# One traced order for every engine queue, with five to eight raw weight buffers and LayerNorm in place, in a two-layer encoder

## The chip, the core and the metric

The kernel runs on one core of a Trainium2 chip. The metric is the device time of one execution, in microseconds. Before the change the median of three runs is 1156.98 us (1156.47 to 1160.61). The execution that the profiler recorded took 1159.23 us, 2.25 us more than that median; all rows below come from it.

## What is computed

Two layers on x (256 tokens, 1024 channels). Each layer is a half-step SwiGLU FFN (inner width 2816), a token mixer, and a second half-step FFN, each followed by a LayerNorm of the scaled residual. The mixer of layer 0 is multi-scale pooling, that of layer 1 a dilated attention with 16 heads of 64 in three dilation groups.

```python
def reference(x, ...):
    for i in range(DEPTH):
        h = _swiglu(x, ffn1_w_gate[i], ffn1_w_up[i], ffn1_w_down[i])
        x = _layer_norm(ALPHA * x + MACARON_WEIGHT * h, ln_gain[i, 0], ln_bias[i, 0])
        if i % N_MIXERS == 0:
            m = _pool_mixer(x, pool_w_in[p], pool_w_group[p], pool_scale[p], pool_w_out[p])
        else:
            m = _dilated_attention_mixer(x, attn_w_qkv[a], attn_w_out[a])
        x = _layer_norm(ALPHA * x + m, ln_gain[i, 1], ln_bias[i, 1])
        h = _swiglu(x, ffn2_w_gate[i], ffn2_w_up[i], ffn2_w_down[i])
        x = _layer_norm(ALPHA * x + MACARON_WEIGHT * h, ln_gain[i, 2], ln_bias[i, 2])
    return x
```

## The kernel before

Every product is taken in three parts: each float32 operand is split into a rounded high half and the remainder, and high times high, high times low and low times high are added in PSUM. For the weights this happens on the chip. A **unit** of weights is 128 x 2048 numbers and arrives in two **half blocks** of 128 x 1024 (512 KB): SyncE (SP) issues the load into a buffer `raw` (L109), ScalarE (ACT) casts it to the high half (L84), VectorE (DVE) subtracts that from `raw` to get the low half (L85), and only then may `raw` take the next load. There are three `raw` buffers (`N_RAW = 3`), four places `w` for split units, three `d` and one `dlast` for the down weights of an FFN.

An FFN loops over 22 blocks f of 128 inner channels. A block takes one `gate/up` unit: 16 wide products (`mm_wide`, L124 with 512 columns and L125 with 256), eight into one PSUM bank for the gate and eight into another for the up part. `join` copies half of a bank to SBUF on ACT (L129) and adds the other half on DVE (L130); then come the SiLU on ACT, the multiplication on DVE and the split into `hTh` and `hTl`. The banks called `mm` are two, so the products of the next block wait until the `join` of the block before has read its bank. The down products (`down`, three instructions each, L116 to L118, made by `mm3`) of an earlier block stand between the wide ones. The first block of the first FFN takes a transposed copy of x, which `load_first` brings in five pieces (one, one, two, two and two eighths), each with the same eighths of the first unit.

In the attention, each pair of heads has its wide products for q and k, and the values of pairs 2 to 7 are products of three instructions. `scores`, `transposed` and `weighted` of a pair are put off and run a given number of products later (`AT_LEFT`, `stepped`), that is, among the values of the next pair. The cleared halves of `kbh` and `kbl` hold the keys of groups 1 and 2. The last pair has no next one: its score products, transposes and weighted sums come when the loop has ended, ahead of `project_out`.

The order of the instructions is the tile scheduler's: it takes the program text as priorities and moves an instruction past others that are not ready in its own simulation, on each engine by itself.

Of the kernel before, what the change touches and what calls it, by code (L numbers as in the profile page):

```python
# [40 lines left out]
N_RAW = 3  # L41


AT_PROJ = (KT, KT + 1)
N_EARLY = 0
# [5 lines left out]


def _alibi(h):
    return 2.0 ** (-8.0 * (h + 1) / (N_GROUPS * N_HEADS))


@with_exitstack
def tile_trunk(ctx: ExitStack, tc: tile.TileContext, x, x_t, ffn_gu, ffn_d, ln_p, pool_in, pool_group,
               pool_scale, pool_out, attn_qk, attn_v, attn_out, ident_c, dist_c, qscale_c,
               window_c, out):  # L60
    nc = tc.nc

    const = ctx.enter_context(tc.tile_pool(name="const", bufs=1))
    wpool = ctx.enter_context(tc.tile_pool(name="wpool", bufs=4))
    xpool = ctx.enter_context(tc.tile_pool(name="xpool", bufs=1))
    lnpool = ctx.enter_context(tc.tile_pool(name="lnpool", bufs=2))
    small = ctx.enter_context(tc.tile_pool(name="small", bufs=4))
    psum = ctx.enter_context(tc.tile_pool(name="psum", bufs=2, space=PSUM))

    def bank(tag):  # L70
        return psum.tile([P, 512], F32, tag=tag, name=tag, bufs=4 if tag == "acc" else 2)

    def banks():
        return [bank("acc") for _ in range(2)]

    ident = const.tile([P, P], F32, name="ident")
    neg_half = const.tile([P, 1], F32, name="neg_half")
    nc.vector.memset(neg_half, -0.5)


    def split(hi, lo, src, scale=None):

        if scale is None:
            return (nc.scalar.copy(out=hi, in_=src),  # L84
                    nc.vector.tensor_tensor(out=lo, in0=src, in1=hi.bitcast(F32), op=ALU.subtract))  # L85
        return (nc.scalar.activation(out=hi, in_=src, func=AF.Copy, scale=scale),
                nc.vector.scalar_tensor_tensor(out=lo, in0=src, scalar=scale, in1=hi.bitcast(F32),
                                               op0=ALU.mult, op1=ALU.subtract))

    @contextmanager  # L90
    def behind(instructions):

        with ExitStack() as bctx:
            for ins in instructions or ():
                bctx.enter_context(tc.issue_after(ins.ins))
            yield

    def load_unit(src, pool=None, tag="w", n=2048, cuts=1):

        pool = pool or wpool  # L100
        both = pool.tile([P, 2, 2048], F32R, tag=tag, name=tag)
        hi, lo = both[:, 0], both[:, 1]
        half = n // 2
        for i in range(2):
            raw = wpool.tile([P, 1024], F32, tag="raw", name="raw", bufs=N_RAW)
            for j in range(cuts):
                r = slice(j * half // cuts, (j + 1) * half // cuts)
                s = slice(i * half + r.start, i * half + r.stop)
                nc.sync.dma_start(out=raw[:, r], in_=src[:, s])  # L109
                split(hi[:, s], lo[:, s], raw[:, r])  # L110
        return hi, lo

    def mm3(o, lhs, rhs, first, last):

        (lh, ll), (rh, rl) = lhs, rhs
        nc.tensor.matmul(o, lhsT=lh, rhs=rh, start=first, stop=False)  # L116
        nc.tensor.matmul(o, lhsT=lh, rhs=rl, start=False, stop=False)  # L117
        nc.tensor.matmul(o, lhsT=ll, rhs=rh, start=False, stop=last)  # L118

    def mm_wide(o, w, xs, first, last):  # L120


        wh, wl = w
        nc.tensor.matmul(o, lhsT=wh, rhs=xs, start=first, stop=False)  # L124
        nc.tensor.matmul(o[:, S:], lhsT=wl, rhs=xs[:, :S], start=False, stop=last)  # L125

    def join(out, o):

        nc.scalar.copy(out=out, in_=o[:, S:])  # L129
        nc.vector.tensor_tensor(out=out, in0=o[:, :S], in1=out, op=ALU.add)  # L130

    def ln_params(i):
        gb = lnpool.tile([P, 2, D], F32, tag="gb", name="gb", bufs=1)
        nc.sync.dma_start(out=gb, in_=ln_p[i:i + 1].broadcast_to([P, 2, D]))
        return gb

    def new_xT():

        xT = xpool.tile([P, KT, 2 * S], F32R, tag="xT", name="xT")
        return xT[:, :, :S], xT[:, :, S:], xT  # L140

    def transpose_x(y, xT, tt, b):

        ts = slice(tt * P, (tt + 1) * P)
        bs = slice(b * 4, (b + 1) * 4)
        tr = bank("tr").rearrange("p (k t) -> p k t", k=4)
        for k in range(4):
            c = b * 4 + k
            nc.tensor.transpose(tr[:, k, :], y[:, c * P:(c + 1) * P], ident)
        return split(xT[0][:, bs, ts], xT[1][:, bs, ts], tr)  # L150

    def layer_norm(acc, weight, before, gb):
# [4 lines left out]
        y = lnpool.tile([P, D], F32, tag="y", name="y", bufs=4)  # L157
        least = min(a.shape[1] for a in acc)
        stats = small.tile([P, 4, 6], F32, tag="stats", name="stats", bufs=2)
        pieces = []  # L160
        at = 0
        for a in acc:
            s = slice(at, at + a.shape[1])
            pieces.append(s)
            nc.vector.scalar_tensor_tensor(out=y[:, s], in0=before[:, s], scalar=ALPHA / weight, in1=a,
                                           op0=ALU.mult, op1=ALU.add)
            for c in range(s.start, s.stop, least):
                nc.vector.bn_stats(out=stats[:, c // least, :], in_=y[:, c:c + least])
            at = s.stop
        mv = small.tile([P, 2], F32, tag="mv", name="mv")  # L170
# [615 lines left out]
```

## Time and profile before

| | us |
|---|---|
| median of three runs | 1156.98 |
| the profiled execution | 1159.23 |
| its span | 1157.5 |
| TensorE busy (PE) | 1108.6 |
| VectorE busy (DVE) | 777.0 |
| ScalarE busy (ACT) | 623.2 |
| mean granted clock of TensorE, share of full speed | 0.992 |

By the timeline, the stages stand at about: FFN of layer 0 4 to 203 us, pooling to 250 and its output projection to 275, second FFN to 465, first FFN of layer 1 to 661, attention to 937, its output projection to 960, last FFN to 1150. Busy shares are averages over these stages. A row of the timeline ends with the idle time of the engine just before the instruction and what ended it. Products overlap by their fill time, so a stretch in which TensorE is shown fully busy can still hold short waits.

### The profile page before, as it was taken

To read this page: it belongs to the slowest core of one execution; us is meant where nothing else is said; L and a number is where in the kernel's file an instruction comes from. 1 tells how busy PE (TensorE), PEld (TensorE's weight loads), DVE (VectorE), ACT (ScalarE), POOL (GpSimd) and SP (SyncE) were. 2 spreads that over 40 slices of the span, in tenths; PEclk is the share of its full clock that TensorE was granted. 3 is DMA by queue.
4 is the path that set the end of the run, shared out by engine and by line. 5 is a ranking of instruction groups with operands and counts; after the bars stand their busy time and mean duration, and the time that the engine had idled before them with its cause. 6 is when DMAs were issued, how large, how long until landed. Compare 5 with 4: busy or idle time off the path is not lost.

```text
span 1157.5 us, 16223 instructions
## 1 busy us (share of the span) xinstructions
PE 1108.6 (96%) x6164; PEld 950.3 (82%) x6164; DVE 777.0 (67%) x1341; ACT 623.2 (54%) x1130; POOL 16.5 (1%) x32
## 2 busy tenths in 40 slices
PE   7989989999999999999998999999999999999997
PEld 6878878878778877988887897988988878888876
DVE  6676657578665656666556659888888877656555
ACT  5665454254554553455445358777777745545440
POOL 0000000000000000000000110000000000000000
PEclk9999989999999999999999999999999999999999
DMA  8765554165655554465555344444445436655421
GB/s 274 255 237 200 200 180 166 57 216 205 223 202 190 181 179 150 145 236 201 176 188 183 123 143 167 141 147 140 142 155 167 151 117 218 227 200 181 171 104 37
DMA packets 57534, 201.80 MB, mean 174 GB/s; under 512 B 6640, under 2 KB 7536, under 8 KB 56688
## 3 DMA queue, kind: packets, MB, share of 16 engines
q1 hardware_dynamic: 57456, 200.77, 50.8%
q8 instruction: 48, 0.79, 0.3%
q14 instruction: 30, 0.25, 0.1%
HBM read 199.70 MB, written 1.05 MB: 173 GB/s over the span
## 4 chain that ended last, share of the span: by engine, by line
DMA 31%; PE 27%; ACT 18%; DVE 18%; issue 6%; SPq 0%; DVEq 0%; ACTq 0%
DMA raw<-in_ffn_d_dram 15%; DMA raw<-in_ffn_gu_dram 14%; DVE w L85 8%; PE mm L124 7%; ACT w L84 7%; ACT d L84 4%; PE mm L125 4%; DVE d L85 3%; PE acc L116 3%; PE acc L118 3%; PE acc L117 3%; PE mm L118 1%; PE mm L117 1%; PE mm L116 1%; DMA raw<-in_pool_out_dram 1%
## 5 line engine op out<-in xcount | busy, mean ns | idle before, releaser
L124 PE MATMUL mm<-xT,w 128*128 128x512 f32 x1456 | 529.9, 405 | 30.8 <-DVE up L130 18.8
L125 PE MATMUL mm<-xT,w 128*128 128x256 f32 x1456 | 410.5, 283 | 0.3 <-DVE w L85 0.3
L85 DVE TENSOR_TENSOR w<-raw,w 128x1024 fp32r<-128x1024 f32 (+3 forms) x277 | 322.7, 1173 | 86.2 <-ACT w L84 81.5
L124 PEld LDWEIGHTS mm<-xT,w 128*128 128x128 f32 x1456 | 276.7, 190 | 107.7 <-DVE up L130 24.8
L84 ACT CAST w<-raw 128x1024 fp32r<-128x1024 f32 (+3 forms) x277 | 275.6, 1010 | 81.8 <-DMA raw<-in_ffn_gu_dram 63.8
L125 PEld LDWEIGHTS mm<-xT,w 128*128 128x128 f32 x1456 | 279.0, 192 | 2.5 <-DVE w L85 0.6
L85 DVE TENSOR_TENSOR d<-raw,d 128x1024 fp32r<-128x1024 f32 x100 | 122.0, 1225 | 163.7 <-ACT d L84 163.0
L84 ACT CAST d<-raw 128x1024 fp32r<-128x1024 f32 x100 | 104.4, 1049 | 146.8 <-DMA raw<-in_ffn_d_dram 132.7
L118 PE MATMUL acc<-d,hTl 128*128 128x512 f32 (+1 forms) x316 | 121.7, 385 | 1.0 <-DVE hTl L85 1.0
L116 PE MATMUL acc<-d,hTh 128*128 128x512 f32 (+1 forms) x316 | 122.1, 386 | 0.0
L117 PE MATMUL acc<-d,hTh 128*128 128x512 f32 (+1 forms) x316 | 121.6, 385 | 0.0
L118 PEld LDWEIGHTS acc<-d,hTl 128*128 128x128 f32 x316 | 59.3, 188 | 14.6 <-DVE hTl L85 2.5
L124 PE MATMUL acc<-xT,w 128*128 128x512 f32 x192 | 70.4, 402 | 0.0
L116 PEld LDWEIGHTS acc<-d,hTh 128*128 128x128 f32 x316 | 59.4, 188 | 13.1 <-ACT hTh L84 0.3
L246 ACT ACTIVATE h<-h 128x256 f32<-128x256 f32 x79 | 32.9, 417 | 68.9 <-DVE h L130 68.9
L117 PEld LDWEIGHTS acc<-d,hTh 128*128 128x128 f32 x316 | 59.4, 188 | 10.0
L130 DVE TENSOR_TENSOR up<-mm,up 128x256 f32<-128x256 f32 x79 | 33.3, 421 | 38.7 <-ACT up L129 38.7
L116 PE MATMUL mm<-w,xT 128*128 128x384 f32 (+1 forms) x176 | 56.9, 323 | 0.6 <-ACT v L508 0.3
L117 PE MATMUL mm<-w,xT 128*128 128x384 f32 (+1 forms) x176 | 56.5, 321 | 0.0
L118 PE MATMUL mm<-w,xT 128*128 128x384 f32 (+1 forms) x176 | 56.5, 321 | 0.0
L125 PE MATMUL acc<-xT,w 128*128 128x256 f32 x192 | 54.2, 282 | 0.0
L84 ACT CAST hTh<-h 128x256 fp32r<-128x256 f32 x79 | 31.9, 404 | 29.5 <-DVE h L247 29.5
(168 smaller groups left out, 1385.0 us busy)
## 6 DMA issues: line engine op xcount, KB each, us to landing
raw<-in_ffn_gu_dram SPq DMA_DIRECT2D x172, 512.0 KB, 4.5
raw<-in_ffn_d_dram SPq DMA_DIRECT2D x88, 512.0 KB, 4.2
raw<-in_attn_qk_dram SPq DMA_DIRECT2D x48, 512.0 KB, 3.8
raw<-in_attn_v_dram SPq DMA_DIRECT2D x32, 384.0 KB, 3.2
gb<-in_ln_p_dram SPq DMA_DIRECT2D x6, 1024.0 KB, 4.8
raw<-in_pool_in_dram SPq DMA_DIRECT2D x8, 512.0 KB, 3.6
raw<-in_pool_out_dram SPq DMA_DIRECT2D x8, 512.0 KB, 4.7
raw<-in_attn_out_dram SPq DMA_DIRECT2D x8, 512.0 KB, 3.7
```

What stands on the lines that cost most here:

```text
L84: return (nc.scalar.copy(out=hi, in_=src), nc.vector.tensor_tensor(out=lo, in0=src, in1=hi.bitcast(F32), op=ALU.subtract))
L85: nc.vector.tensor_tensor(out=lo, in0=src, in1=hi.bitcast(F32), op=ALU.subtract))
L116: nc.tensor.matmul(o, lhsT=lh, rhs=rh, start=first, stop=False)
L117: nc.tensor.matmul(o, lhsT=lh, rhs=rl, start=False, stop=False)
L118: nc.tensor.matmul(o, lhsT=ll, rhs=rh, start=False, stop=last)
L124: nc.tensor.matmul(o, lhsT=wh, rhs=xs, start=first, stop=False)
L125: nc.tensor.matmul(o[:, S:], lhsT=wl, rhs=xs[:, :S], start=False, stop=last)
L130: nc.vector.tensor_tensor(out=out, in0=o[:, :S], in1=out, op=ALU.add)
L246: nc.scalar.activation(out=out, in_=ps_g, func=AF.Silu)
```

## The change

The tile scheduler is switched off (`manual_schedule`): each engine issues in the order in which the program traces its instructions. A class `Order` decides that order with a timeline of its own. The products are traced in program order. Before each of them, everything that starts earlier by that timeline is traced: **jobs** (the copies, joins, activations and splits that follow a product) and weight operations. A cast or subtract of weights is passed over while a job of the same engine is due before 0.4 of its duration has gone. Weights are one list for the whole program; loads, casts and subtracts follow the list, each as far ahead as buffers allow.

The `raw` buffers become five, with three more (`rawx`) in the FFN and projection stages. The place `dlast` is gone, and units of gate/up weights may lie in `w` or `d`. LayerNorm writes over the residual in two tiles `y` instead of four. Products and their arithmetic are the same. The diff touches the whole file; this is its core:

```diff
-N_RAW = 3
+N_RAW = 5
+N_RAW_MORE = 3
...
+class Order:
...
+    def _next(self):
+        best = None
+        soon = {}
+        for j in self.jobs:
+            engine, us, fn = j.ops[j.at]
+            if any(not a.done for a in j.after):
+                continue
+            start = max([self.free[engine], j.ready] + [a.ready for a in j.after])
+            soon[engine] = min(soon.get(engine, 1e9), start)
+            if best is None or start < best[0]:
+                best = (start, 0, lambda j=j, start=start: self._job(j, start))
+        for start, engine, us, fn in self._weights():
+            if engine in soon and soon[engine] < start + 0.4 * us:
+                continue
+            if best is None or start < best[0]:
+                best = (start, 1, fn)
+        return best
...
+    def need(self, *jobs):
+        for j in jobs:
+            if j is not None:
+                self.until(lambda: j.done)
+                self.pe = max(self.pe, j.ready)
...
+    def product(self, us, fn):
+        self.advance(self.pe)
+        fn()
+        self.pe += us
...
+    ctx.enter_context(tc.manual_schedule())
...
-            raw = wpool.tile([P, 1024], F32, tag="raw", name="raw", bufs=N_RAW)
...
-        y = lnpool.tile([P, D], F32, tag="y", name="y", bufs=4)
...
-            last_place = fctx.enter_context(tc.tile_pool(name="dlast", bufs=1, side="right", reuse_waits="tile"))
...
+        raw_x, raw_w = q.raws[0:2], q.raws[2:4]
+        for ks in (1, 1, 2, 2, 2):
...
+            nc.sync.dma_start(out=rx, in_=x_t[:, s])
+            nc.sync.dma_start(out=rw, in_=ffn_gu[0, 0][:, s])
...
+            j = job(ops[0], ops[2], ops[1], ops[3])
...
+            if at == 1024 or at == 2048:
+                need(j)
+                raw_x[at // 1024 - 1].free = raw_w[at // 1024 - 1].free = j.ready
```

What this moves, at three places.

**The start, SP's queue.** `x_t` is the transposed input, `ffn_gu` the gate/up weights and `ffn_d` the down weights of the first FFN. Before:

```order
L670 DMA y<-in_x_t_dram 128x256
L671 DMA raw<-in_ffn_gu_dram 128x256
L670 DMA y<-in_x_t_dram 128x256
L671 DMA raw<-in_ffn_gu_dram 128x256
L670 DMA y<-in_x_t_dram 128x512
L671 DMA raw<-in_ffn_gu_dram 128x512
L670 DMA y<-in_x_t_dram 128x512
L671 DMA raw<-in_ffn_gu_dram 128x512
L670 DMA y<-in_x_t_dram 128x512
L671 DMA raw<-in_ffn_gu_dram 128x512
L109 DMA raw<-in_ffn_gu_dram 128x512 x4
L109 DMA raw<-in_ffn_d_dram 128x1024 x2
```

After:

```order
L952 DMA raw_87<-in_x_t_dram 128x256
L953 DMA raw_89<-in_ffn_gu_dram 128x256
L952 DMA raw_87<-in_x_t_dram 128x512
L953 DMA raw_89<-in_ffn_gu_dram 128x512
L161 DMA raw_91<-in_ffn_gu_dram 128x1024
L161 DMA rawx_110<-in_ffn_gu_dram 128x1024
L161 DMA rawx_111<-in_ffn_d_dram 128x1024
L161 DMA rawx_112<-in_ffn_d_dram 128x1024
L952 DMA raw_88<-in_x_t_dram 128x512
L953 DMA raw_90<-in_ffn_gu_dram 128x512
L952 DMA raw_88<-in_x_t_dram 128x512
L953 DMA raw_90<-in_ffn_gu_dram 128x512
```

Four half blocks of the second gate/up unit and the first down unit now stand ahead of the last two pieces of the input and of the first unit (x_t 128x512 twice, ffn_gu 128x512 twice). ACT and DVE have their four casts and subtracts at the same place of their queues.

**The attention, TensorE, the scores of one token half of a pair among the values of the next pair** (`kbh`, `kbl` are the split keys of groups 1 and 2, `mm<-w,xT` a values product). Before:

```order
L117 MATMUL acc<-kbl_5732,qh 128x2x128
L118 MATMUL acc<-kbh_5731,ql 128x2x128
L116 MATMUL mm<-w,xT 128x384
L116 MATMUL acc<-kbh_5737,qh 128x2x128
L117 MATMUL mm<-w,xT 128x384
L118 MATMUL mm<-w,xT 128x384
L116 MATMUL mm<-w,xT 128x384
L117 MATMUL mm<-w,xT 128x384
L118 MATMUL mm<-w,xT 128x384
L116 MATMUL mm<-w,xT 128x384
L117 MATMUL mm<-w,xT 128x384
L117 MATMUL acc<-kbl_5738,qh 128x2x128
```

After:

```order
L775 MATMUL acc_78<-k_5830,qh_5792 128x256
L777 MATMUL acc_78<-k_5830,q0l_5022 128x256
L775 MATMUL acc_78<-k_5830,qh_5792 128x256
L777 MATMUL acc_78<-k_5830,q0l_5022 128x256
L318 MATMUL acc_75<-kbh_5010,qh 128x2x128
L319 MATMUL acc_75<-kbl_5011,qh 128x2x128
L320 MATMUL acc_75<-kbh_5010,ql 128x2x128
L318 MATMUL acc_75<-kbh_5016,qh 128x2x128
L319 MATMUL acc_75<-kbl_5017,qh 128x2x128
L320 MATMUL acc_75<-kbh_5016,ql 128x2x128
L318 MATMUL mm_80<-w_85,xT 128x384
L319 MATMUL mm_80<-w_85,xT 128x384
```

Before, eight instructions of values products stand between the score products of group 1 (`kbl_5732` is its low part) and the `kbl` product of group 2, one of them ahead of that group's first product. Now the six score products of groups 1 and 2 are next to each other, and the values products come after them. This is pair 2; pairs 3 to 6 read alike, and in pairs 0 and 1 the six stand next to each other in both kernels.

**The end of the attention, TensorE, the last pair** (`mm<-w,oTh` is a product of `project_out`, `tr<-ident,s` a transpose, `tr<-ph,v` a weighted sum). Before:

```order
L116 MATMUL mm<-w,oTh_5702 128x512
L117 MATMUL mm<-w,oTh_5702 128x512
L116 MATMUL acc<-kbh_5725,qh 128x2x128 x2
L118 MATMUL mm<-w,oTl_5703 128x512
L116 MATMUL mm<-w,oTh_5704 128x512
L117 MATMUL mm<-w,oTh_5704 128x512
L118 MATMUL mm<-w,oTl_5705 128x512
L116 MATMUL mm<-w,oTh_5706 128x512
L117 MATMUL acc<-kbl_5726,qh 128x2x128
L118 MATMUL acc<-kbh_5725,ql 128x2x128
L117 MATMUL acc<-kbl_5726,qh 128x2x128
L118 MATMUL acc<-kbh_5725,ql 128x2x128
```

After:

```order
L820 MATMUL tr_81<-ident,s 128x128 x3
L835 MATMUL tr_82<-ph,v_7444 128x256
L835 MATMUL tr_82<-pl,v_7444 128x256
L835 MATMUL tr_82<-ph,v_7509 128x256
L844 MATMUL tr_82<-p_7723,v_1_5029 64x64 x4
L835 MATMUL tr_82<-pl,v_7509 128x256
L835 MATMUL tr_82<-ph,v_7444 128x256
L835 MATMUL tr_82<-pl,v_7444 128x256
L835 MATMUL tr_82<-ph,v_7509 128x256
L844 MATMUL tr_82<-p_7726,v_1_5029 64x64 x4
L835 MATMUL tr_82<-pl,v_7509 128x256
L318 MATMUL mm_79<-w_86,oTh_4984 128x512
```

Before, twelve products of `project_out` stand between the last pair's scores, transposes and weighted sums, and three of their instructions already between its scores. Now the first one comes when the last weighted sum has been issued.

## Rows read from the trace of the kernel before

**Rows 1.** Page, part 1: busy time, share of the span, instructions of each engine.

```profile
PE 1108.6 (96%) x6164; PEld 950.3 (82%) x6164; DVE 777.0 (67%) x1341; ACT 623.2 (54%) x1130; POOL 16.5 (1%) x32
```

**Rows 2.** Waits of TensorE: instruction waiting <- releaser: us in total, times, longest us.

```profile
PE mm L124 <- DVE up L130: 18.8, 15, 3.2
...
PE mm L124 <- DVE h L130: 4.6, 8, 1.5
...
PE acc L116 <- ACT kbh L643: 1.6, 4, 0.7
...
PE acc L117 <- DVE kbl L646: 1.2, 1, 1.2
```

**Rows 3.** Timeline, two wide products one after the other (line, form).

```profile
156.29 0.40 PE L124 MATMUL mm<-xT,w 128*128 128x512 f32 x1
...
156.64 0.39 PE L124 MATMUL mm<-xT,w 128*128 128x512 f32 x1
```

**Rows 4.** Timeline, 160 to 168 us: start us, us, engine, line, [idle before <-releaser].

```profile
160.07 7.49 SPq L109 DMA_DIRECT2D raw<-in_ffn_d_dram  x2
...
164.90 1.04 ACT L84 CAST d<-raw 128x1024 fp32r<-128x1024 f32 x1 [3.73 <-DMA raw<-in_ffn_d_dram]
...
167.59 0.80 PE L124 MATMUL mm<-xT,w 128*128 128x512 f32 x1 [3.16 <-DVE up L130]
```

**Rows 5.** Timeline, after another wait of the same kind, in the last FFN.

```profile
1113.63 0.50 PE L124 MATMUL mm<-xT,w 128*128 128x512 f32 x1 [2.44 <-DVE up L130]
```

**Rows 6.** Windows: us, busy of PE, PEld, DVE, ACT, POOL; PEclk, DMA share, GB/s.

```profile
8.00:10.00 2.00, 1.70 (x5) 1.53 (x6) 2.00 (x4) 1.89 (x4) 0.00 (x0) 1.00 1.01 370
166.40:173.20 6.80, 5.61 (x17) 4.84 (x18) 5.63 (x8) 3.86 (x7) 0.00 (x0) 0.50 0.63 212
627.20:630.60 3.40, 3.40 (x12) 2.84 (x11) 2.56 (x5) 1.78 (x4) 0.00 (x0) 0.50 0.76 259
709.10:712.50 3.40, 3.40 (x13) 2.92 (x12) 3.05 (x14) 3.23 (x7) 0.00 (x0) 0.50 0.51 204
1113.60:1120.40 6.80, 6.77 (x38) 5.89 (x39) 5.56 (x9) 3.58 (x8) 0.00 (x0) 1.00 0.22 77
920.00:940.00 20.00, 19.84 (x113) 15.04 (x111) 14.13 (x47) 10.08 (x25) 0.00 (x0) 1.00 0.32 103
```

**Rows 7.** Timeline of the start, around the fifth eighth of the first product.

```profile
8.14 0.62 ACT L84 CAST xT<-y 128x512 fp32r<-128x512 f32 x1
...
9.72 0.63 PE L124 MATMUL mm<-xT,w 128*128 128x512 f32 x1
```

**Rows 8.** Timeline, second-group scores next to the first's: pairs 0 (707) and 1 (731).

```profile
707.08 0.39 PE L116 MATMUL acc<-kbh,qh 128*128 128x256 f32 x1 [0.67 <-ACT kbh L643]
...
708.72 0.39 PE L117 MATMUL acc<-kbl,qh 128*128 128x256 f32 x1 [1.25 <-DVE kbl L646]
...
731.23 0.29 PE L117 MATMUL acc<-kbl,qh 128*128 128x256 f32 x1
```

**Rows 9.** Timeline, pair 2: the same key product with a values product before it.

```profile
762.28 0.39 PE L116 MATMUL acc<-kbh,qh 128*128 128x256 f32 x1 [0.46 <-ACT kbh L643]
```

**Rows 10.** Timeline, TensorE through the last pair of the attention.

```profile
921.34 0.28 PE L125 MATMUL acc<-xT,w 128*128 128x256 f32 x1
...
933.54 0.52 PE L549 MATMUL tr<-ident,s 128*128 128x128 f32 x3
...
936.53 0.68 PE L569 MATMUL tr<-p,v 128*64 128x64 f32 x8
```

**Rows 11.** Timeline, one project_out product of three and the next one's start.

```profile
943.17 0.39 PE L116 MATMUL acc<-w,oTh 128*128 128x512 f32 x1
...
943.87 0.39 PE L116 MATMUL acc<-w,oTh 128*128 128x512 f32 x1
```

**Rows 12.** Page, part 5: group xcount | busy us, mean ns | idle before, releaser.

```profile
L85 DVE TENSOR_TENSOR d<-raw,d 128x1024 fp32r<-128x1024 f32 x100 | 122.0, 1225 | 163.7 <-ACT d L84 163.0
...
L130 DVE TENSOR_TENSOR up<-mm,up 128x256 f32<-128x256 f32 x79 | 33.3, 421 | 38.7 <-ACT up L129 38.7
```

More of the change, by code (lines that the diff above doesn't have):

```diff
@@ L90, in behind @@
[L90 to L104, printed above, removed]
-            raw = wpool.tile([P, 1024], F32, tag="raw", name="raw", bufs=N_RAW)
[L106 to L111, printed above, removed]
+    gb = lnpool.tile([P, 2, D], F32, name="gb")
@@ new lines, in finish_last, with gu_unit, d_unit @@
+    def finish_last(steps, weight):
+        for tt in range(2):
+            ln = LayerNorm(ys[tt], weight, 512 if tt == 0 else 256)
+            for b in steps(tt):
+                if b is not None:
+                    ln.piece(*b)
+            for s, done in zip(ln.pieces, ln.end()):
+                need(done)
+                nc.sync.dma_start(out=out[tt * P:(tt + 1) * P, s], in_=ys[tt][:, s])
+    def gu_unit(i, f):
+        return Unit(ffn_gu[i, f], 2048, ("w", "d"))
+    def d_unit(i, f):
+        return Unit(ffn_d[i, f], 2048, ("d",) if f > (NFF - N_HELD) // 2 - 1 else ("d", "w"))
@@ L328, in ffn @@
-                    join(up, parts[1])
-                    gate(h, up, h)
-                    split(hT[f][0], hT[f][1], h)
-                down_unit(f)
-                if f == 6:
-                    gb = ln_params(n_ln)
-                    if first:
-                        load_x(ys)
-                while n_major <= f and done < min(f, NFF - N_HELD):
-                    for tt in range(2):
-                        for j in range(len(acc[tt])):
-                            down(done, tt, j)
-                    done += 1
@@ new lines, in ffn @@
+            hT[f] = places[f % n_places]
+            ready[f] = job(dve(S, lambda h=h: nc.vector.tensor_tensor(out=h, in0=h, in1=up, op=ALU.mult)),
+                           *split(*hT[f], h, S), after=jobs)
+            if f == 6:
+                ln_params(n_ln)
+                if first:
+                    load_x()
+            while n_major <= f and done < min(f, NFF - N_HELD):
+                for tt in range(2):
+                    for j in range(len(acc[tt])):
+                        down(done, tt, j)
+                done += 1
@@ L361, in steps, with project_out @@
+        def steps(tt):
+            for j in range(len(acc[tt])):
+                for f in range(NFF - N_HELD, NFF):
+                    down(f, tt, j)
+                    if f < NFF - 1:
+                        yield None
+                yield (acc[tt][j], cuts[tt][j]) if last else acc[tt][j]
+        if last:
+            return finish_last(steps, 0.5)
+        return finish(steps, 0.5, (N_HELD, N_HELD + 1))
+    def project_out(units, lhs, lhs_done, i, early):
+        ln_params(i)
         def steps(tt):
@@ new lines, in scores, with transposed @@
+            return soft
+        def transposed(s, s_done, tt, h, ph, ph_done):
+            ts = slice(tt * P, (tt + 1) * P)
+            b = bank("tr")
+            need(s_done)
+            tr = b.tile[:, :384].rearrange("p (n q) -> p n q", n=3)
+            for n in range(3):
+                product(0.109, lambda: nc.tensor.transpose(tr[:, n, :], s[:, n * P:(n + 1) * P], ident))
+            b.readers.append(job(*split(ph[h][0][:, :, ts], ph[h][1][:, :, ts], tr[:, 0:2, :], 256),
+                                 act(P, lambda: nc.scalar.copy(out=ph[h][2][:, tt], in_=tr[:, 2, :]))))
+            ph_done.append(b.readers[-1])
@@ L663, in load_first @@
+        while left:
+            left.pop(0)[1]()
+        return oT, o_done
+    first_unit = Unit(ffn_gu[0, 0], 2048, ("w",))
+    first_in = {}
+    def load_first():
+        slot = next(s for s in q.slots if s.kind == "w")
+        first_unit.slot, slot.free = slot, None
+        hi, lo = slot.tile[:, 0], slot.tile[:, 1]
+        raw_x, raw_w = q.raws[0:2], q.raws[2:4]
         at = 0
```

1114 lines of the change are left out of this document (671 added, 443 removed).

## The prediction, made before the changed kernel ran

> **What bounds the kernel now.** I read the page first. TensorE is shown busy in 96% of the span [rows 1], so its own work is the floor, and since the products stay the same, only its waits, its clock and the idle time around them can change. The list of its waits comes second. The largest entries by far are the joins of the FFN: the next block's first wide product stands until DVE has read the bank, 15 times for `up` and 8 times for `h`, 18.8 + 4.6 = 23.4 us in all [rows 2].
>
> The timeline shows how such a wait arises. At 160.07 SP issues a load for the down weights; only then had one of the three `raw` buffers come free. ACT, in order, sits idle 3.73 us until that half block lands, and its cast begins at 164.90. The copy for the join is queued behind the cast, and TensorE resumes at 167.59 after 3.16 us [rows 4]. So the chain is: a late subtract frees `raw` late, the load starts late, an in-order cast waits for it, and a copy that was ready waits behind the cast. DVE tells the same: its subtracts of `d` alone were preceded by 163.7 us of idle time that the casts ended [rows 12].
>
> Third come the windows for TensorE's clock. After the wait at 164 the granted clock is 0.50 in a stretch of 6.8 us (the lower of its two levels, 1.2 GHz), and at 627 in one of 3.4 us; TensorE was busy 5.61 and 3.40 us in them, and half of that, 2.8 + 1.7 = 4.5 us, is lost [rows 6]. The stretch from 1113.6, which follows a wait of the same kind of 2.44 us, stands at 1.00 [rows 5, 6].
>
> **What goes.** With eight buffers for raw half blocks in the FFNs a load is issued up to eight blocks ahead instead of three, and the order lets a job (the copy and the add of a join) pass a cast that would begin shortly before it. I take the 23.4 us as gone but for 2 us, for the block after each stage boundary, where the places `w` and `d` are all taken; the bound from below is nothing kept, from above 6 us, about two waits of the size of the one at 164 [rows 4]. The first product after a wait runs 0.50 us instead of 0.39 [rows 5, 11], so 23 waits take another 23 x 0.11 = 2.5 us along. The two stretches at the lower clock go with the waits that stand ahead of them, 4.5 us. **FFN: -23.4 - 2.5 - 4.5 + 2 = -28.4 us.** What would be late next there is a cast that waits for a place; TensorE releases one every few us, so I price that within the 2 us.
>
> **What comes at the start.** Four half blocks, 4 x 512 KB = 2.1 MB, now stand on SP's queue ahead of the last two pieces of the input. The DMA engines are full there (share 1.01, 370 GB/s [rows 6]), so these pieces land 2.1 MB / 370 GB/s = 5.7 us later. Before, ACT casts the first of the two at 8.14 and TensorE takes it at 9.72 [rows 7]; now about 15.4. The four casts and subtracts in front of it (1.04 and 1.23 us each [rows 4, 12], 4.2 and 4.9 us together) run while the blocks land, one every 1.4 us, and end little later. Nothing gives these 5.7 us back: TensorE works without large waits in the following blocks, so early weights are worth nothing to them. From below 3.5 us, if the rest of the first block, whose products take 0.63 us there [rows 7], runs at 0.39 when it comes 6 us later: eight pairs, 0.29 us each. From above 7.5 us, if a stretch of 3.4 us more runs at the lower clock. I take **+5.7**, by the landing.
>
> **What comes in the attention.** In pairs 2 to 6 the score products of group 2 now follow those of group 1 at once. Strict order has a price that the trace shows twice: pair 0 waits 0.67 + 1.25 = 1.92 us for the split keys, pair 1 not at all [rows 8]. With a values product in between, pair 2 pays 0.46 us [rows 9]. In pairs 2 to 6 the keys come late as in pair 0, because a weight subtract of 1.23 us [rows 12] stands between the join's add and their low parts. I take 1.3 us, nearer to pair 0: 5 x (1.3 - 0.46) = **+4.2 us**; the bounds are 5 x (0 - 0.46) = -2.3 and 5 x (1.92 - 0.46) = +7.3.
>
> The last pair has lost its cover. From the last wide product at 921.34 to the last weighted sum at 937.2 TensorE is full: 19.84 of 20 us [rows 6, 10]. In these 15.9 us stand twelve products of `project_out`, 0.70 us each [rows 11], 8.4 us in all; the pair's own products are the other 7.5. Now these twelve come afterwards. If the pair's chain of keys, scores, exponentials, transposes and splits took as long as before, TensorE would lose 8.4 us. It should be shorter, since no transposes have to wait for their turn between products of 0.7 us; from the first score to the last transpose at 933.54 it is mostly DVE and ACT, one softmax after another. At best it loses half, 4 us. I take **+6 us**, in the middle, as nothing in the rows tells which. Behind it I put one stretch of 3.4 us at the lower clock, **+1.7**, because of three waits with such a stretch behind them one (709) was made of two short waits in the attention [rows 6, 8].
>
> The other parts. LayerNorm writes over the residual, on the same DVE instructions: nothing. Its transposes in the two projections now come at fixed products, where the scheduler had them some products later: +1 us, between 0 and 2. The loads of the LayerNorm parameters no longer wait on SP with weights behind them; by then eight half blocks are in: nothing.
>
> **The sum.** -28.4 + 5.7 + 4.2 + 6 + 1.7 + 1 = -9.8 us against the profiled 1159.23, that is 1149.4. The profiled execution is 2.25 us above the median of the runs, so the forecast is **1147 us** in the runs' terms. The bounds of the parts, added with most of them near their middle, give it 1140 to 1154 as its own range.
>
> **The rivals.**
>
> *The costs are hidden, the gain is whole.* Nothing of the FFN waits stays (-30.4), the start costs 3.5, the last pair 4 with no low clock, the pairs gain 2.3: -25.2 us, 1132 us. For it speaks that the pair at 731 shows strict order without a wait [rows 8]; against it, that the DMA engines are full at the start. 0.18.
>
> *More raw buffers do not do what they should.* If casts are held by the places `w` and `d`, or by ACT's own order, loads run ahead and wait in SBUF, and half the FFN gain stays away: -14.2 + 18.6 = +4.4, 1161 us. Against it speaks the row in which ACT waits for a DMA and for nothing else [rows 4]. 0.12.
>
> *The clock falls after every short wait.* At 707 two waits of 0.67 and 1.25 us were followed by a stretch at 0.50 [rows 6, 8]. If each of the five pairs buys that, 5 x 1.7 = 8.5 us come on top: -1.3, 1156 us. Against it: the wait of 2.44 us at 1113 is longer than both and was followed by 1.00 [rows 5, 6]. 0.12. The Trainium skill, page "TensorE: Matmul & The Clock Gate", section "A second HAM failure mode: psum-queue depth-cycling", states such a rule: short idle times between groups of products can make the clock swing between its levels, and the slow stretches are paid again and again. It speaks against this change; by it the time would be this rival's, while the row at 1113.6 disagrees with it, and so I give it no more.
>
> *Jobs behind weight work, in every FFN block.* This one ends slower. Each queue is now fixed by an assumed timeline. If that runs off from the chip's, a join's copy (about 0.42 like the add) can stand behind a cast of 1.04 and its add behind a subtract of 1.23 [rows 4, 12], together 3.11 us, while the other bank gives TensorE 8 x 0.35 = 2.8 us of cover [rows 3]. Each join so hit costs 0.31 us. There are 2 x 79 = 158 [rows 12]; from 50 of them on the kernel is slower by over 0.5%, and with half of them hit it loses 24 us: +15, 1172 us. For it: nothing on the chip can correct the order. Against it: a weight operation is passed over when a job is due, and a queue that runs late shifts all its work alike. 0.15.
>
> **The numbers.** A measurement of this kernel can tell about 0.5%, 5.8 us, from no change: 1151.2 to 1162.8 is "same". The forecast has 0.43; its own range lies mostly below 1151.2, so 0.30 of that is faster and 0.13 same. The hidden costs add 0.18 faster. Of the idle buffers 0.08 is same and 0.04 slower; of the clock 0.03 faster, 0.08 same and 0.01 slower; of the jobs 0.02 same and 0.13 slower. Together: faster 0.51, same 0.31, slower 0.18. The range runs from near the hidden-cost case to where the jobs' case begins to bite, **1133 to 1165**, with about one in ten left out on each side.
>
> **What would show it.** The waits for `up` and `h` should be down to some 2 us, with no casts of `d` waiting for a DMA inside the FFNs; the product at 9.72 should come at about 15.4; the score products of pairs 2 to 6 should wait for `kbl`; and TensorE should show about 6 us of idle time between the attention's last wide product and `project_out`. The forecast is wrong if waits for `up` remain in numbers, if the first block ends where it did, or if the stretch of the last pair stays full.

## The result, and the profile after

The changed kernel takes 1129.92 us (1129.05 to 1130.47), the kernel before 1157.91 us beside it: a ratio of 0.9755 (0.9734 to 0.9776), 28 us or 2.4% faster. The forecast was 1147 with a range of 1133 to 1165: the right direction, too small a gain.

The page of the change, parts 1 and 4 (busy time by engine; the chain that ended last), and two groups of part 5:

```profile
PE 1095.1 (97%) x6164; PEld 954.4 (85%) x6164; DVE 777.2 (69%) x1339; ACT 628.1 (56%) x1128; POOL 16.2 (1%) x32
...
PE 93%; DVE 4%; ACT 1%; DMA 1%; issue 1%; SPq 0%; DVEq 0%; ACTq 0%
...
L183 DVE TENSOR_TENSOR d<-raw,d 128x1024 fp32r<-128x1024 f32 x81 | 96.6, 1218 | 3.8 <-ACT d L174 3.8
...
L174 ACT CAST d<-raw 128x1024 fp32r<-128x1024 f32 x81 | 82.9, 1048 | 6.0 <-DMA raw<-in_window_dram 5.1
```

Before, DVE's subtracts of `d` were preceded by 163.7 us of idle time [rows 12]; now those from `raw` by 3.8. Of the FFNs' weight supply hardly anything is late any more: TensorE waits four times for `d`, 1.2 us in all, near the end of the first and of the last FFN. The chain is TensorE's own work for 93% of the span. TensorE's waits by releaser, of the change:

```profile
PE mm L330 <- DVE xT L307: 11.0, 3, 5.2
PE acc L319 <- DVE kbl L924: 3.8, 6, 0.7
PE tr L820 <- DVE s L811: 3.8, 4, 1.5
PE acc L319 <- DVE w L183: 2.9, 2, 2.8
PE acc L318 <- ACT kbh L921: 1.4, 1, 1.4
...
PE acc L319 <- DVE d L183: 1.2, 4, 0.4
PE mm L330 <- DVE h L338: 0.5, 1, 0.5
```

`up`, first of the list before [rows 2], is gone from it, and of `h` 0.5 us is left. Almost all that remains stands at the start (`xT`, of which 4.2 us are the time ahead of the first product, as in the kernel before), in the attention (`kbl`, `kbh`, `s`) and at the pooling (`w`).

For a table by stage I count TensorE's products and transposes, 6164 in every trace and in nearly the same order, and take the start of the same one in each timeline: before the change the 1st, 301st, 901st, 1301st, 3301st, 4691st, 5001st and last stand at 4.2, 66.8, 190.8, 270.9, 653.4, 885.6, 937.4 and 1150.0 us, after it at 4.2, 73.5, 184.7, 268.9, 628.6, 856.9, 917.9 and 1120.9. "FFNs" are the stretches from the 301st to the 901st, the 1301st to the 3301st and the 5001st to the last, the rest of the attention's projection among them. In us:

| stage | before | forecast of the change in it | after |
|---|---|---|---|
| start | 62.6 | +5.7 | 69.3 |
| FFNs | 719.2 | -28.4 | 674.0 |
| end of the first FFN, pooling, its projection | 80.1 | +1 | 84.2 |
| attention, to the last pair | 232.2 | +4.2 | 228.3 |
| last pair, start of the projection | 51.8 | +7.7 | 60.9 |
| sum | 1145.9 | -9.8 | 1116.7 |

The FFNs gave 45.2 us, where 28.4 were forecast. The costs forecast for the start and the last pair are there; the attention ahead of the last pair became 3.9 us shorter, where 4.2 more were forecast.

The start. Timeline before, the first product of the fifth eighth (start us, us, engine, line, [idle before <-releaser]):

```profile
11.00 1.05 PE L124 MATMUL mm<-xT,w 128*128 128x512 f32 x2
```

Timeline of the change:

```profile
14.77 0.61 ACT L306 CAST xT<-raw 128x512 fp32r<-128x512 f32 x1
...
16.86 0.76 PE L330 MATMUL mm<-xT,w 128*128 128x512 f32 x1 [5.24 <-DVE xT L307]
...
22.71 0.50 PE L330 MATMUL mm<-xT,w 128*128 128x512 f32 x1 [0.51 <-DVE h L338]
```

The fifth eighth of x is cast at 14.77 instead of 8.14 [rows 7] and multiplied at 16.86 instead of 11.00, 5.9 us later. (An eighth has four instructions, so the fifth begins with the 17th product, at 11.00; the product at 9.72, which [rows 7] and the prediction take for it, is the 13th and belongs to the fourth.) The last pair, TensorE only:

```profile
892.47 0.28 PE L331 MATMUL acc<-xT,w 128*128 128x256 f32 x1
...
894.94 0.38 PE L318 MATMUL acc<-kbh,qh 128*128 128x256 f32 x1 [1.36 <-ACT kbh L921]
...
900.25 0.55 PE L820 MATMUL tr<-ident,s 128*128 128x128 f32 x3 [1.49 <-DVE s L811]
...
902.73 0.88 PE L820 MATMUL tr<-ident,s 128*128 128x128 f32 x3 [1.01 <-DVE s L811]
...
904.51 0.88 PE L820 MATMUL tr<-ident,s 128*128 128x128 f32 x3 [0.91 <-DVE s L811]
...
909.46 0.39 PE L318 MATMUL mm<-w,oTh 128*128 128x512 f32 x1
```

From the last wide product to the first product of the projection 17.0 us pass, with waits for `kbh`, `kbl` and four times for the softmax. The clock in this stretch, after the pairs' short waits, after the pooling's wait and after the start's (windows: us, busy of PE, PEld, DVE, ACT, POOL, then PEclk, DMA share, GB/s):

```profile
732.00:735.40 3.40, 2.74 (x15) 2.54 (x16) 3.34 (x12) 2.02 (x2) 0.00 (x0) 1.00 0.81 268
...
895.70:902.40 6.70, 4.02 (x18) 3.25 (x18) 6.50 (x31) 3.98 (x11) 0.00 (x0) 0.75 0.62 215
902.50:909.20 6.70, 5.56 (x29) 4.51 (x29) 4.46 (x10) 2.03 (x7) 0.00 (x0) 0.50 0.29 90
209.60:212.90 3.30, 3.30 (x9) 2.29 (x8) 3.03 (x3) 0.00 (x0) 0.00 (x0) 0.50 0.73 240
15.00:21.80 6.80, 4.93 (x15) 4.13 (x16) 4.75 (x6) 3.18 (x5) 0.00 (x0) 0.50 1.03 409
```

### The profile page after: what moved, and what is told of

The parts are those of the page before. It is cut to its first block, busy times and chain, and to the rows that moved or that the text cites. A ratio compares the mean times of both kernels' runs of the same rounds, so it can differ in the third digit from the quotient of the medians.

```text
span 1128.6 us, 16092 instructions
## 1 busy us (share of the span) xinstructions
PE 1095.1 (97%) x6164; PEld 954.4 (85%) x6164; DVE 777.2 (69%) x1339; ACT 628.1 (56%) x1128; POOL 16.2 (1%) x32
## 3 DMA queue, kind: packets, MB, share of 16 engines
HBM read 199.70 MB, written 1.05 MB: 178 GB/s over the span
## 4 chain that ended last, share of the span: by engine, by line
PE 93%; DVE 4%; ACT 1%; DMA 1%; issue 1%; SPq 0%; DVEq 0%; ACTq 0%
PE mm L330 30%; PE mm L331 15%; PE acc L319 8%; PE acc L320 8%; PE acc L318 8%; PE mm L320 4%; PE mm L319 4%; PE mm L318 4%; PE acc L330 4%; PE acc L331 2%; DVE w L183 1%; PE tr L835 1%; PE tr L844 1%; PE tr L820 1%; DMA rawx<-in_ffn_d_dram 1%; PE tr L352 1%
## 5 line engine op out<-in xcount | busy, mean ns | idle before, releaser
L330 PE MATMUL mm<-xT,w 128*128 128x512 f32 x1104 | 395.6, 399 | 11.5 <-DVE xT L307 11.0
L331 PE MATMUL mm<-xT,w 128*128 128x256 f32 x1104 | 311.7, 282 | 0.0
L330 PEld LDWEIGHTS mm<-xT,w 128*128 128x128 f32 x1104 | 209.1, 189 | 59.2 <-ACT w L306 11.9
L183 DVE TENSOR_TENSOR w<-raw,w 128x1024 fp32r<-128x1024 f32 (+1 forms) x187 | 217.8, 1177 | 15.5 <-ACT w L174 14.7
L331 PEld LDWEIGHTS mm<-xT,w 128*128 128x128 f32 x1104 | 210.7, 191 | 1.9 <-DVE w L307 0.5
L174 ACT CAST w<-raw 128x1024 fp32r<-128x1024 f32 (+1 forms) x187 | 186.6, 1017 | 4.7 <-DMA raw<-in_ffn_gu_dram 1.3
L330 PE MATMUL mm<-xT,d 128*128 128x512 f32 x352 | 125.3, 397 | 0.0
L331 PE MATMUL mm<-xT,d 128*128 128x256 f32 x352 | 98.9, 281 | 0.0
L319 PE MATMUL acc<-d,hTh 128*128 128x512 f32 (+1 forms) x228 | 88.4, 388 | 1.2 <-DVE d L183 1.2
L318 PE MATMUL acc<-d,hTh 128*128 128x512 f32 (+1 forms) x228 | 88.5, 388 | 0.0
L330 PEld LDWEIGHTS mm<-xT,d 128*128 128x128 f32 x352 | 66.2, 188 | 15.8
L183 DVE TENSOR_TENSOR w<-rawx,w 128x1024 fp32r<-128x1024 f32 (+1 forms) x63 | 75.0, 1206 | 6.0 <-ACT w L174 6.0
L331 PEld LDWEIGHTS mm<-xT,d 128*128 128x128 f32 x352 | 66.1, 188 | 0.5
```

Source lines behind the costliest of these rows:

```text
L174: self.nc.scalar.copy(out=slot.tile[:, 0, half * n:(half + 1) * n], in_=raw[:, :n])
L183: self.nc.vector.tensor_tensor(out=u.slot.tile[:, 1, s], in0=r.tile[:, :n], in1=u.slot.tile[:, 0, s].bitcast(F32), op=ALU.subtract)
L330: nc.tensor.matmul(o, lhsT=wh, rhs=xs[:, k], start=first, stop=False)
L331: nc.tensor.matmul(o[:, S:], lhsT=wl, rhs=xh[:, k], start=False, stop=last)
```

## The experiments

Two theories stood at first. **Depth**: the FFN waits went because loads run further ahead than three half blocks. **Order**: they went because each queue is traced in one order in which jobs lead. Each run is timed beside the kernel before on the same chip. That kernel took 1157 us on one chip and 1167 to 1169 on others, so ratios to it differ a little from chip to chip; the change itself was not run on another chip, but the second FFN (the 1301st to the 2301st) takes 180.9 to 181.0 us in its trace and in those of e5 to e13, on four chips. Between the scheduler's kernels the chip counts: the FFNs of e3, which is the kernel before but for LayerNorm in place, take 728.9 us on the chip of e1 to e4, those of the kernel before 719.2 on its own. So e1 and e4 are read against e3.

**Three raw buffers in the fixed order** (e1).

```diff
-N_RAW = 5
-N_RAW_MORE = 3
+N_RAW = 4
+N_RAW_MORE = 0
...
                 q.release(first_unit)
+                q.retire(q.raws[3:])
```

> The change, with three raw buffers from the second block on (four while the first block loads, none more in the FFNs). Depth theory (the FFN waits went because loads run more than three half blocks ahead): most of the 45 us that the four FFNs gained come back, the time is 1160 to 1175 us against 1130 for the change. Order theory (they went because each queue is traced in one order in which jobs lead): 1126 to 1135 us, and the waits for up and h stay under 3 us.

1183.94 us, a ratio of 1.0146 (1.0113 to 1.0179): slower than the kernel before. Its largest waits:

```profile
PE mm L331 <- DVE w L183: 24.7, 25, 5.7
PE mm L330 <- ACT w L174: 7.0, 4, 2.8
PE acc L318 <- ACT kbh L922: 5.4, 6, 1.7
```

TensorE waits for the weights themselves, 25 times; the joins are next to nothing. The FFNs take 702.4 us, 26.5 less than with three buffers in the scheduler's order on the same chip (e3); the attention loses, 253.9 us against 234.0 there and 228.3 with the change. So the order theory is wrong as to the kernel, and depth is needed, but the joins' waits are taken away by the order even then. The FFNs differ: the second takes 180.9 us, the same as with eight buffers, while the first is 18.1 us longer than the change's (129.3 against 111.2), the third 7.0 and the last 3.3.

**Weights that do not give way to jobs** (e2).

```diff
-            if engine in soon and soon[engine] < start + 0.4 * us:
-                continue
```

> The change, without the rule that a weight cast or subtract gives way to a job that is due before 0.4 of its duration has gone; whichever can start first is traced first. Depth theory: 1129 to 1134 us, joins come at most one cast and one subtract later and the second bank covers that. Order theory: waits for up and h come back in numbers, 1145 us or more.

1167.53 us, 1.0005 (0.9988 to 1.0023): all that the change had gained is gone, but not where the order theory looked for it:

```profile
PE tr L350 <- DVE y L394: 12.1, 5, 4.3
PE acc L316 <- ACT kbh L919: 11.1, 6, 2.3
PE acc L317 <- DVE kbl L922: 7.7, 7, 1.2
...
PE mm L328 <- DVE h L336: 0.6, 1, 0.6
```

The joins (`h` 0.6 us) are covered by the second bank. The LayerNorms (`y`) and the attention's keys are not: there a job is one link of a chain for which TensorE stands. The attention takes 248.9 us and its last pair 66.3; the FFNs 684.1. The price per join of the slower rival in the prediction is therefore not paid.

**The scheduler's kernel with LayerNorm in place, three and five raw buffers** (e3, e4).

```diff
-        y = lnpool.tile([P, D], F32, tag="y", name="y", bufs=4)
+        y = before
...
-        raw_x = [lnpool.tile([P, D], F32, tag="y", name="y", bufs=4) for _ in range(2)]
+        raw_x = ys
...
-    ys = [lnpool.tile([P, D], F32, tag="y", name="y", bufs=4) for _ in range(2)]
+    ys = [lnpool.tile([P, D], F32, tag="y", name="y", bufs=2) for _ in range(2)]
...
-N_RAW = 3
+N_RAW = 5
```

(e3 leaves the last two lines out.)

> The kernel before, with LayerNorm written over the residual (two y tiles instead of four, the first pieces of the input go into the y tiles), still three raw buffers and the scheduler's order. Both theories: no change, 1154 to 1162 us, since the same DVE instructions run. If the waits at the stage boundaries came from the y tiles, some 5 us less.

> The kernel before with LayerNorm in place and five raw buffers, in the scheduler's order. Depth theory: two more raw buffers take most of the waits for up and h (23 us listed, some 45 us with what hangs on them), 1115 to 1138 us. Order theory: the scheduler still puts casts ahead of copies, 1152 to 1160 us.

e3: 1169.86 us, 1.0024 (1.0006 to 1.0041). LayerNorm in place gives nothing by itself; it gives the room for the buffers. e4: 1124.49 us, 0.9641 (0.9615 to 0.9667). Two more buffers in the old order make more than the whole change (45.4 us beside e3, on the same chip). Its waits:

```profile
PE mm L124 <- DVE h L130: 10.3, 6, 2.8
PE mm L124 <- ACT w L84: 4.4, 1, 4.4
...
PE acc L116 <- ACT kbh L643: 0.8, 4, 0.3
```

`up` is gone, `h` has still 10.3 us. The FFNs take 687.7 us: depth alone takes 41.2 off the 728.9 of e3, and the fixed order 13.7 more, down to the change's 674.0. Taken the other way round, the order alone gives 26.5 (e3 to e1) and depth 28.4 more. Each alone takes a large part of the waits away, and neither takes all. But the scheduler's start (61.4), pooling (79.1) and last pair (51.7) are shorter than the change's by 7.9, 5.1 and 9.2 us.

**The input first** (e5): no load, cast or subtract of other weights is traced while the five pieces are.

```diff
     def _weights(self):
+        if self.hold:
+            return
...
     def load_first():
+        q.hold = True
...
+        q.hold = False
         q.pe = first_in[0].ready
```

> The change, with the five pieces of the input and the first unit ahead of every other load, cast and subtract. Theory (the start's cost is paid in full and earns nothing later): the first block ends where it did before the change, 6.5 to 7.5 us less than the change, a ratio of about 0.969 beside its 0.9755. Rival (the four early half blocks save waits in the first FFN): less than 3 us gained, 0.973 or more.

1118.46 us, 0.957 (0.9556 to 0.9584). 64.5 us at the start, 4.8 less than the change, where 6.5 to 7.5 were expected; the first FFN behind it stays at 111.1. The 1.9 us that are left against the kernel before are waits in the second block that the change has not or has shorter, 1.2 us for `h` and 1.4 for a subtract of `w`, so the early blocks had earned a little. The run is better than expected by a gain elsewhere: 5.1 us more go at the beginning of the pooling, which the edit does not touch. The placement there hangs on the order's own clock, and it moved; which instruction made the difference was not followed further.

**Products of the projection in the last pair's chain** (e6).

```diff
             leave(p, qs, ks_, qk_done)
+        begun = project_steps(a_out, oT, o_done, KT - 1)(0)
+        for n in COVER:
+            for _ in range(n):
+                next(begun)
+            left.pop(0)[1]()
         while left:
             left.pop(0)[1]()
```

(`COVER` is 4, 0, 3, 1, 2, 2, 2, and `project_out` goes on with `begun`)

> The change, with fourteen products of the attention's output projection set between the last pair's scores, transposes and weighted sums (four ahead of the first scores, then 0, 3, 1, 2, 2, 2). Theory (the last pair's chain is bare and lasts about 17 us of which TensorE works 7.5): 8 to 9.5 us less than the change, a ratio of about 0.968. Rival (the chain is held by DVE and ACT, whose weight work for the next stage would then be late): less than 4 us gained, 0.972 or more.

1135.34 us, 0.9712 (0.9697 to 0.9726): 5 us slower than the change. The place of it:

```profile
903.87 0.80 PE L320 MATMUL mm<-w,oTh 128*128 128x512 f32 x1 [4.38 <-DVE w L184]
...
917.97 0.50 PE L319 MATMUL mm<-w,oTh 128*128 128x512 f32 x1 [2.04 <-ACT oTh L307]
```

```profile
902.59 1.23 DVE L184 TENSOR_TENSOR w<-raw,w 128x1024 fp32r<-128x1024 f32 x1
```

The covering products asked for the third weight unit, whose subtract the order had put behind the softmax at 902.59, and stood 4.38 us for it with the transposes behind them. Even so the last pair's stage is 2.6 us shorter than the change's (58.3); 6.1 us are lost behind it, where TensorE waits 2.04 us for `oTh` and 2.9 for a subtract of `d`. So the rival was right that weight work comes late, and the theory that the chain can be covered; e11 takes other products.

**Scores two products later** (e7).

```diff
-AT_LEFT = (2, 9, 18, 21, 27, 30, 40)
+AT_LEFT = (4, 11, 18, 21, 27, 30, 40)
```

> The change, with a pair's scores put off by two products more (AT_LEFT begins 4, 11 instead of 2, 9). Theory (the five pairs each wait 0.92 us for kbl because the scores come too early): these waits go, 3.5 to 4.6 us less than the change, a ratio of about 0.972. Rival (the transposes behind them come at the same products and then wait for the softmax): no gain, 0.975.

1125.82 us, 0.9634 (0.9619 to 0.9649): 4.1 us less than the change. The stretch of the pairs behind the first (the 3701st to the 4691st product) is 4.1 shorter. The wait for `kbl` falls from 3.8 to 0.5 us:

```profile
PE acc L319 <- DVE kbl L924: 0.5, 1, 0.5
```

**A shorter transfer in the order's own timeline** (e8).

```diff
-    DMA_US, LANDING_US, LAG = 2.5, 2.6, 0.2
+    DMA_US, LANDING_US, LAG = 1.5, 2.6, 0.2
```

> The change, with 1.5 us instead of 2.5 us per half block in the order's own timeline of transfers. Theory (at the start of the pooling two weight subtracts stand behind LayerNorm because the order believes their data later than it is): the wait of 2.8 us there and the slow stretch behind it go, 4 to 5 us less than the change, a ratio of about 0.972. Rival (DVE is full there, 14 of 16 us, and any order is late): within 2 us of the change.

1125.67 us, 0.963 (0.9614 to 0.9646). The first part of the pooling (the 901st to the 1001st product) takes 21.8 us instead of 28.0: the wait there was the order's, not a full DVE's. The value alone is not shown to be its cause, since e5 and e9 keep 2.5 us and take 22.9 and 22.8 there.

**Five raw buffers everywhere** (e9).

```diff
-N_RAW_MORE = 3
+N_RAW_MORE = 0
```

> The change, with five raw buffers everywhere (the three more in the FFN and projection stages left out). If depth counts up to eight: the FFNs lose 10 us or more of the 45 they gained, 1140 us or more. If five half blocks ahead are enough, as the scheduler's kernel with five suggests: 1127 to 1135 us.

1118.08 us, 0.9582 (0.9532 to 0.9631), 12 us faster than the change with eight and 9 below what was expected. The FFNs take 673.9 us, the same as with eight. The start takes 62.9 us, since only one half block finds a buffer ahead of the input, and the pooling 77.6. Its start in the timeline, beside that of the change above:

```profile
10.21 0.62 ACT L306 CAST xT<-raw 128x512 fp32r<-128x512 f32 x1
...
12.31 0.47 PE L330 MATMUL mm<-xT,w 128*128 128x512 f32 x1 [1.49 <-DVE xT L307]
```

and, of its waits, the one in the pooling, 2.8 us with the change:

```profile
PE acc L319 <- DVE w L183: 0.7, 1, 0.7
```

So the three further buffers are worth nothing in the FFNs and cost what stands in the start's term, 6.4 us. Another 6.6 go in the pooling, as in e5; what moved the order there was not followed.

**Three edits together, and with a cover from two units** (e10, e11). e10 takes e5, e7 and e8; e11 adds e6's edit with the projection's first two weight units only and `COVER = (3, 0, 2, 1, 1, 1, 0)`.

> The change with the input first, scores two products later and 1.5 us per half block in the order's own timeline, all three together. If their gains stand beside each other (start 4.8, pooling 5 to 6, scores 4.1 us in the stages where each alone changed the trace): 1112 to 1116 us. If the pooling's gain is one and the same in two of them and the rest interferes: 1117 us or more.

> The three together, and eight products of the output projection, of its first two weight units only, set into the last pair's chain (3, 0, 2, 1, 1, 1, 0). Theory (the chain can be covered as long as the covering products need no weights that are split during it): 5 us less than the three together. Rival (what is gained there is lost in the next FFN, whose first weights can only be loaded when the attention's buffers are given back): within 2 us of the three together.

e10: 1118.44 us, 0.9584 (0.9543 to 0.9626), 2.4 us above the upper end of what was expected. The scores and the pooling give what they gave alone, the start does not:

```profile
18.14 1.04 ACT L178 CAST d<-rawx 128x1024 fp32r<-128x1024 f32 x1 [0.23 <-DMA rawx<-in_ffn_d_dram]
19.09 0.37 ACT L341 COPY h<-mm 128x256 f32<-128x256 f32 x1
...
19.97 0.50 PE L334 MATMUL mm<-xT,w 128*128 128x512 f32 x1 [4.14 <-DVE h L342]
```

Four casts stand ahead of the first join's copy. Their data is late, and TensorE waits 4.14 us: the very chain of [rows 4], made by a fixed order. At 1.5 us per half block the order has the input and the first unit, four half blocks' worth, landed 8.6 us after its start (4 x 1.5 + 2.6); in the trace the cast of their last piece waits until 12.98. Neither edit alone does this: e5 and e8 wait 1.2 and 1.1 us for `h` there. e11: 1111.67 us, 0.9526 (0.9484 to 0.9567). The last pair's stage falls to 52.5 us and the FFN behind it keeps 203.8 against 203.1: the cover holds when its products need nothing that is split during the chain.

**The version of the parts** (e12: five buffers, scores later, the cover of e11; the order's own times as in the change) **and four buffers** (e13: `N_RAW = 4`, `N_RAW_MORE = 0`).

> The change with five raw buffers everywhere, scores two products later, and eight products of the output projection in the last pair's chain (3, 0, 2, 1, 1, 1, 0). From the stages of the runs that had each alone: 1118 for five buffers, less 4.1 for the scores, less 7 to 8 for the end: 1105 to 1108 us. If the parts interfere: 1110 us or more.

> The change with four raw buffers everywhere. Depth theory by supply (a half block takes about 7 us from its load to its subtract's end, so three buffers give one per 2.3 us, four one per 1.75, and an FFN block needs three in 8.4 us): four are enough in the FFNs, each within 2 us of the change's, 1118 to 1130 us. Depth theory by distance (loads must run five ahead): the FFNs stand between those with three and with five, 1140 us or more.

e12: 1106.48 us, 0.9474 (0.9446 to 0.9502), faster than both kernels, as the stages of the single runs add up. Its two largest waits are the start's and the softmax's:

```profile
PE mm L331 <- DVE xT L308: 6.2, 3, 4.2
PE tr L820 <- DVE s L811: 2.1, 3, 1.3
```

e13: 1121.7 us, 0.9605 (0.9571 to 0.9639); the FFNs take 673.5 us. Four buffers are enough there in the fixed order and three are not. The expectation's estimate of the need holds: three half blocks per block of 8.4 us (sixteen wide products at 0.35, four of three parts at 0.70), one per 2.8 us. Its 7 us per buffer are too short for three buffers: in the first FFN of e1 a half block holds its buffer for 8.9 us on the mean (4.9 from issue to landing, 1.1 until the cast begins, 1.05, 0.6 until the subtract, 1.2), in the second for 8.4. Three buffers then give one per 2.96 and per 2.8 us, which is just the need or less, and nothing is left to make up for a late start. How much of that holding time is the place that the order gives the casts, with its 2.5 us per half block, and not the number of buffers, is open: three buffers were not run with a shorter time.

| stage, us | before | e3, 3, scheduler | e1, 3 | e13, 4 | e9, 5 | change, 8 | e4, 5, scheduler | e12 |
|---|---|---|---|---|---|---|---|---|
| start | 62.6 | 63.5 | 65.6 | 64.3 | 62.9 | 69.3 | 61.4 | 64.1 |
| FFNs | 719.2 | 728.9 | 702.4 | 673.5 | 673.9 | 674.0 | 687.7 | 673.4 |
| pooling | 80.1 | 78.8 | 86.0 | 77.9 | 77.6 | 84.2 | 79.1 | 77.6 |
| attention | 232.2 | 234.0 | 253.9 | 229.5 | 228.4 | 228.3 | 230.5 | 224.9 |
| last pair | 51.8 | 51.8 | 63.0 | 62.4 | 60.4 | 60.9 | 51.7 | 52.5 |

## Why the prediction was wrong

**The step that failed is the FFN term**, "-23.4 - 2.5 - 4.5 + 2 = -28.4 us"; it measured -45.2. The mechanism, loads further ahead and jobs that pass casts, was the right one (e1, e4), the size was not. With -45.2 in the place of -28.4 the prediction's own sum gives -26.6; the stages of the traces add up to -29.2. I took the listed waits of two releasers and 0.11 us behind each. Taking, for each product of the FFN stages in the trace of before, the distance to the next one's start less the usual distance for its width (about 231 ns for 512 columns, 117 to 118 for 256), one gets about 48 us in all: 26.4 at waits for `up` and `h`, 4.2 at the lower clock, 7.7 at waits for other releasers, and some 10.5 in about 95 delays that are too short to be listed as idle time. The same sum for the change is about 3. A nanosecond in the usual distance moves either sum by about 2 us and their difference, 45.2, not at all. So three parts of the term were short: the waits themselves by 3.0, the short delays by 8.0, and the waits for `hmh`, `hm` and the like, behind each LayerNorm, which I had left out altogether, though the list of before has them:

```profile
PE acc L116 <- ACT hmh L84: 1.9, 2, 1.3
...
PE mm L124 <- DVE hm L247: 1.4, 3, 0.7
...
PE acc L118 <- DVE hTl L85: 1.0, 3, 0.6
```

And the 2 us that I let stay after each stage boundary did not stay as such. The sum of idle times was the wrong measure: the loss of a stage is its length less that of the same products at their usual distance.

**The start: right, from a misread row.** +5.7 forecast, +6.7 measured. The fifth eighth comes 5.9 us later, as the landing had it, but from 11.00 and not from 9.72, so the "about 15.4" of the prediction was 1.3 too early. The upper bound's reason came true too: the clock is at 0.50 from 15.0 to 21.8 in the change, and all sixteen products of 512 columns in the first block take 0.5 us or more, where before they take 0.40 from 12.87 on. So the second block begins 7.35 us late (22.71 instead of 15.36). Nearly nothing of it comes back: with one early block instead of four the start takes 62.9 us and the first FFN the same 111.1 (e9).

**The pairs: the mechanism right, the size too large.** +4.2 forecast. `kbl` is waited for in five pairs, 0.66 us each, where I took 1.3; the products with short delays of their own became fewer, and the stretch of the pairs behind the first, with four of these waits, grew by 1.0 us (157.3 to 158.3). What I had not seen is that pair 0's two waits [rows 8] and the stretch at 0.50 behind them [rows 6] go: its stage, the 3301st to the 3701st, shrank by 4.9 (74.9 to 70.0). e7 shows that the waits that are left are those of scores that come too early.

**The last pair: right in kind, a little short.** +6 and +1.7 forecast, +9.1 measured. About 0.7 of it is the fifth wait for `kbl` (at 863.11), which falls into this stage; the rest is the bound of 8.4 at which the twelve products were priced without any cover. The waits listed are 5.7 us, where about 6 were forecast, and the lower clock is granted for longer than the one stretch of 3.4 us: 0.75 on the mean from 895.7 to 902.4 and 0.50 from 902.5 to 909.2. How the 8.4 divide between the chain and the clock no run separates.

**The pooling: too small.** +1 forecast for both projections, +4.1 measured here. Two weight subtracts stand behind LayerNorm on DVE, and TensorE waits 2.77 us:

```profile
206.87 2.35 DVE L183 TENSOR_TENSOR w<-raw,w 128x1024 fp32r<-128x1024 f32 x2
```

```profile
208.14 0.50 PE L319 MATMUL acc<-w,xT 128*128 128x512 f32 x1 [2.77 <-DVE w L183]
```

I had counted the transposes that move, not the queue they share with the weights. In e5 and e8, without this wait, the stage takes 77.7 us, less than before the change.

**The rivals.** The time falls beside the first one (1132), but not by its reason: its costs were not hidden, the gain was larger. That more buffers do nothing is refuted by e4. Jobs behind weight work in every block did not happen (e2: `h` 0.6 us with no rule at all). The clock after every short wait did not come either: after the pairs' waits of 0.66 us it stays at 1.00, in the window from 732 on and behind the other four. Longer waits of the same pairs do bring it: in e2, with 1.77 us for `kbh` and 1.23 for `kbl` in each, a stretch at 0.50 follows in three of the five. The rule of the Trainium skill, page "TensorE: Matmul & The Clock Gate", section "A second HAM failure mode: psum-queue depth-cycling", that short idle times between groups of products swing the clock, agrees with this trace for the last pair (0.50 from 902.5 to 909.2, after waits of 1.36 and 1.49 us and during one of 1.01) and not for the five pairs.

## What to carry to other kernels

Size the gain of taking stalls away by the length of the stage against the same products at their usual distance, not by the listed waits of one releaser: here the list had 23 of 45 us. When buffers are added and an order is fixed in one change, try them apart: two more buffers in the old order gave more than the whole change, and in the new order four buffers were enough, the last three only let the planner load what nobody waited for ahead of the input. A fixed order is as good as the times it was made with, and it can turn on small shifts of them: in the change it put two subtracts of weights behind a LayerNorm, in e10 a ready copy behind casts without data, and edits elsewhere (e5, e9) took the first away.

## What the runs showed that was not expected

The listed idle time leaves out much of what a wait costs TensorE: about 95 delays of some 0.11 us in the FFNs before, 15 in them after the change, where the products run at their usual distance. The kernel before, whose waits hang on transfers, took 1157 us on one chip and 1167 to 1169 us on others; why is open. With the loads far enough ahead the second FFN took the same time to 0.1 us on each of them. And the granted clock of a window can mislead at the start: before the change it reads 1.00 from 8 to 10 us [rows 6], while the products there take 0.63 us [rows 7], as they do in the change at 0.50.
